# Four transposed quarters and sums behind them, in place of seven transposed operands

## The chip, the cores and the metric

One Trainium2 chip, one of its cores. The metric is the device time of one execution in microseconds; lower is better. A core has a matrix engine (TensorE, PE in the profile; its weight loads are PEld), VectorE (DVE), ScalarE (ACT) and GpSimd (POOL) for elementwise work, and SyncE (SP), whose queue issues most DMAs here.

## The reference

Two sequences, a prompt of 512 rows and a sample of 1024 rows, both 1024 wide, go through one encoder layer with the same weights. The part that matters here is the feed-forward half:

```python
h = _rmsnorm(x, norm_ffn_g[l])
u = _dwconv(h @ w_up[l], ffn_dw_w[l], ffn_dw_b[l])        # 1024 -> 2 x 2816
x = x + (jax.nn.silu(u[..., :D_FF]) * u[..., D_FF:]) @ w_down[l]
```

Everything is float32 in and out.

## The kernel before, in words

Every float32 product is made of three matmuls: each operand is split into a high part (rounded to fp32r, a cast on ACT) and a low part (what is left, one subtraction), and high x high, high x low and low x high are added up in PSUM.

For the sample, the product of the normed rows with `w_up` is made by a scheme of seven block products in place of eight. The rows are cut into four quarters: `rows[t, b]` holds row block `b` (128 rows) of half `t` (0 or 1) of the sequence, and `L` and `R` are its left and right 512 columns. With a11 = (t 0, L), a12 = (t 0, R), a21 = (t 1, L), a22 = (t 1, R), the seven left operands are

| operand | 1 | 2 | 3 | 4 | 5 | 6 | 7 |
|---|---|---|---|---|---|---|---|
| is | a11 | a12 | a12 - s2 | a22 | s1 = a21 + a22 | s2 = s1 - a11 | a11 - a21 |

For the matmuls each is needed transposed, as four chunks `c` of 128 columns by 512 rows, and split: `A[i, c] = (hi, lo)`.

In the kernel before, `scaled(i)` (L1091) forms the scaled row block and, for half 1, three of the four sums on DVE in row layout; `last_sum` forms the fourth, for two of the four row blocks at once and for the others later. `turned(i, get)` (L1121) then turns operand `i`: for each chunk, four PE transposes (one per row block) into one PSUM bank, the cast on ACT and the low part on DVE, both reading the bank (L1127 and, through the helper `sub`, L1074). Operands 1 and 2 are turned while the output projection of the layer's first half is still running (banks `u`); operands 4, 6, 7, 5 and 3 are turned between the first products of `w_up` (banks `t`, four of them).

`prod(out, j, i, ...)` (L1188) is the product of operand `i` with its partner of weight column `j`: four chunks of three matmuls, 12 in all, accumulating in a PSUM half. After each chunk it calls `next(between)`, through which the transposes come in between. `first` to `seventh` are these products with what goes on around them: for instance `sixth(j)` ends with an ACT copy of its result (`u2`), and `seventh(j)` goes on in the same bank. Before `sixth`, a matmul that writes a value to be overwritten (`armed`, L1257) and an ACT copy (L1394) put the result of product 1 into that bank; `arm()` does so for columns 0 and 1 in the course of `fourth(1)`. The banks they write take the place of the four turning banks, which must have been read by then.

The weight operands are made by `sums_up(j)` (sums on DVE) and `split_up(j, ...)` (L1165: a cast on ACT, the low part on POOL). All SBUF tiles come from a list of slots in fixed sizes (`Slots`; kinds q with 4 KB, c, h with 2 KB, d), handed out in the order in which they became free; a new tile waits for the last reader of the one that was in its slot.

The order of instructions on an engine is the compiler's scheduler's, by a model of time, apart from regions that say otherwise:

```python
by_hand = tc.manual_schedule(engines={mybir.EngineType.PE})
```

From L1352 to the end PE runs in the order in which the code emits, the other engines don't. The emitted order of the stage is: first(0), first(1), then second(0), fourth(0), second(1) with the 20 groups of four transposes in between, fourth(1) with the two armings, sixth(0), sixth(1), seventh(0), seventh(1), fifth(0), fifth(1), third(0), first(2), third(1) and so on; from column 2 on a loop over the 22 columns follows, then the down-projection.

Of the kernel before, what the change touches and what calls it, by code (L numbers as in the profile page):

```python
# [108 lines left out]
def tile_hybrid_encoder(ctx: ExitStack, tc: tile.TileContext, xs, rel_bias, norm_attn_g, w_in,  # L109
# [960 lines left out]
    def add(out, a, b, eng=None):  # L1070
        (eng or nc.vector).tensor_tensor(out, a, b, op=ALU.add)

    def sub(out, a, b, eng=None):
        (eng or nc.vector).tensor_tensor(out, a, b, op=ALU.subtract)  # L1074
# [16 lines left out]
    def scaled(i):  # L1091

        t, b = divmod(i - 4, 4)
        x = rows[t, b] = sb.tile([D])
        if t == 0:
            nc.vector.scalar_tensor_tensor(x[:], x1[i][:], rs2[:, i:i + 1], gFb[:], op0=ALU.mult, op1=ALU.mult)
            x1.pop(i)
            return
        for s in (R, L):
            nc.vector.scalar_tensor_tensor(x[:, s], x1[i][:, s], rs2[:, i:i + 1], gFb[:, s], op0=ALU.mult, op1=ALU.mult)  # L1100
        x1.pop(i)
        e = rows[0, b]
        s1 = rows["s1", b] = sb.tile([NT])
        s2 = rows["s2", b] = sb.tile([NT])
        add(s1[:], x[:, L], x[:, R])
        sub(s2[:], s1[:], e[:, L])
        sub(x[:, L], e[:, L], x[:, L])
        if i >= NB - 2:
            last_sum(b)

    def last_sum(b):
        sub(rows[0, b][:, L], rows[0, b][:, R], rows["s2", b][:])

    def block_rows(i, b):
        if i in (1, 2, 3):
            return rows[0, b][:, R if i == 2 else L]
        if i in (4, 7):
            return rows[1, b][:, R if i == 4 else L]
        return rows["s1" if i == 5 else "s2", b][:]

    def turned(i, get):  # L1121
        for c in range(4):
            held, ap = get()
            for b in range(4):
                nc.tensor.transpose(ap[:, b * P:(b + 1) * P], block_rows(i, b)[:, c * P:(c + 1) * P], ident[:])
            hi, lo = A[i, c] = (sb.tile([NT], F32R), sb.tile([NT], F32R))
            nc.scalar.copy(hi[:], ap)  # L1127
            sub(lo[:], ap, hi[:].bitcast(F32))
            held = None
            yield 0.0  # L1130
        key = {6: "s2", 5: "s1", 7: 1, 3: 0}.get(i)
        for b in range(4):
            rows.pop((key, b), None)

    def old_bank():
        b = bank("turn")
# [82 lines left out]
        for half in range(2):  # L1219
            load_up(j, half)  # L1220
    drain(side)
    for b in range(2):
        last_sum(b)
    split_up(0, 1, 2)
    out_blocks(NB - 2, 0)
    split_up(1, 1, 2)
# [42 lines left out]
    def second(j, between=None):  # L1269
        prod(st[j]["x"][:, L], j, 2, False, True, between)  # L1270
# [88 lines left out]
    def chain(*gens):  # L1359
        for g in gens:  # L1360
            yield from g

    def every(n, gen):

        for c in range(4):
            for _ in range((n * (c + 1)) // 4 - (n * c) // 4):
                next(gen, None)
            yield

    turns = chain(*(turned(i, turn_bank) for i in (4, 6, 7, 5, 3)))  # L1370
    firsts = []
    for j in range(2):
        st[j] = dict(x=wide())
# [16 lines left out]
    def arm():  # L1390
        for j in range(2):
# [438 lines left out]
```

## Time and profile before

| | |
|---|---|
| time, median of 3 runs | 1485.7 us (1485.24 to 1486.14) |
| the profiled execution's own time | 1484.85 us |
| its span (first to last instruction) | 1483.1 us |
| PE busy | 1468.5 us, 99% |
| DVE busy | 1118.2 us, 75% |
| ACT busy | 805.5 us, 54% |
| POOL busy | 770.7 us, 52% |

Times inside the execution count from the span's start. A row of the timeline gives the start, the duration, the engine, the line, the operation, what it writes and reads (slot kinds or tensors), and in brackets the idle time before it with what ended it. Matmuls overlap: the distance between two starts is what one costs, not its duration. A row of stretches gives, for each engine, its busy time and number of instructions, then the granted clock of PE, the DMA share and GB/s. The stage of the change lies at about 690 to 780 us.

### The profile page before, as it was taken

Reading aid. Unit: us, or ns where it says so; the run is one execution under the profiler, and the core shown is the slowest. Engines: PE = TensorE matmul, PEld = TensorE weight load, DVE = VectorE, ACT = ScalarE, POOL = GpSimd, SP = SyncE. Lnnn points to the kernel's source line nnn. Section 1 sums busy time; section 2 is a strip of 40 time slices with the busy share of each in tenths; the row PEclk is TensorE's granted clock in tenths of the full one; section 3 lists DMA queues with packets and bytes.
Section 4 is the critical chain, followed back from the end, with each engine's and each line's share of the span. In section 5 each row is a group of like instructions: output and inputs, shape, how many; then the busy total and the mean of one; then the engine's idle time right before and its main releaser. Section 6 shows DMA issues by size and latency. Waiting matters only on the chain.

```text
span 1483.1 us, 19870 instructions
## 1 busy us (share of the span) xinstructions
PE 1468.5 (99%) x6736; PEld 1212.0 (82%) x6736; DVE 1118.2 (75%) x1510; ACT 805.5 (54%) x1424; POOL 770.7 (52%) x689
## 2 busy tenths in 40 slices
PE   9999999999999999999999999999999999999998
PEld 7788887878888888788888888888888888888886
DVE  6877945648988888676868888888886856578774
ACT  7524555567778776653465545445544553433355
POOL 3564453338779766322336666666654251135546
PEclk9999999999999999999999999999999999999999
DMA  9554331844444454663214443333332494356644
GB/s 367 200 151 146 102 107 29 263 142 142 127 137 136 134 178 142 201 225 108 71 58 142 135 135 128 127 130 128 123 126 87 152 326 167 124 188 220 224 163 163
DMA packets 124626, 228.19 MB, mean 154 GB/s; under 512 B 20420, under 2 KB 45764, under 8 KB 124397
## 3 DMA queue, kind: packets, MB, share of 16 engines
q1 hardware_dynamic: 124092, 226.37, 46.6%
q8 instruction: 53, 0.87, 0.2%
q10 hardware_dynamic: 432, 0.56, 0.1%
q14 instruction: 49, 0.39, 0.1%
HBM read 166.83 MB, written 61.10 MB: 154 GB/s over the span
## 4 chain that ended last, share of the span: by engine, by line
PE 89%; DVE 3%; DMA 3%; ACT 2%; POOL 2%; issue 1%; SPq 0%; POOLq 0%; DVEq 0%; ACTq 0%
PE w L1194 8%; PE w L1196 8%; PE w L1195 8%; PE w L1528 7%; PE w L1527 7%; PE w L1526 7%; PE b L315 4%; PE b L317 4%; PE b L316 4%; PE u L315 4%; PE u L317 4%; PE u L316 4%; PE a L692 1%; PE a L650 1%; PE u L796 1%; PE u L798 1%
## 5 line engine op out<-in xcount | busy, mean ns | idle before, releaser
L163 POOL TENSOR_TENSOR q<-q,q 128x1024 fp32r<-128x1024 f32 x66 | 159.2, 2412 | 66.9 <-ACT q L162 42.8
L1074 POOL TENSOR_TENSOR q<-q,q 128x512 fp32r<-128x512 f32 x81 | 116.5, 1445 | 119.4 <-ACT q L1180 117.1
L1074 DVE TENSOR_TENSOR h<-h,h 128x512 fp32r<-128x512 f32 (+1 forms) x152 | 131.9, 897 | 57.6 <-ACT h L1082 23.4
L1526 PE MATMUL w<-h,h 128*128 128x512 f32 x432 | 168.0, 389 | 0.0
L1528 PE MATMUL w<-h,h 128*128 128x512 f32 x432 | 168.0, 389 | 0.0
L1527 PE MATMUL w<-h,h 128*128 128x512 f32 x412 | 160.3, 389 | 0.0
L1194 PE MATMUL w<-h,q 128*128 128x512 f32 x368 | 144.3, 392 | 0.7 <-ACT w L1267 0.4
L1196 PE MATMUL w<-h,q 128*128 128x512 f32 x368 | 143.2, 389 | 0.0
L1195 PE MATMUL w<-h,q 128*128 128x512 f32 x347 | 135.0, 389 | 0.0
L1074 POOL TENSOR_TENSOR h<-h,h 128x512 fp32r<-128x512 f32 (+1 forms) x38 | 53.5, 1411 | 142.4 <-ACT h L1509 117.5
L1082 ACT CAST h<-h 128x512 fp32r<-128x512 f32 x116 | 69.3, 620 | 104.4 <-DVE h L1074 25.8
L315 PE MATMUL b<-h,q 128*128 128x512 f32 x312 | 123.0, 395 | 1.4 <-ACT h L461 0.8
L317 PE MATMUL b<-h,q 128*128 128x512 f32 x312 | 122.5, 393 | 0.0
L316 PE MATMUL b<-h,q 128*128 128x512 f32 x312 | 122.3, 392 | 0.0
L315 PE MATMUL u<-h,q 128*128 128x512 f32 x272 | 106.8, 393 | 0.0
L316 PE MATMUL u<-h,q 128*128 128x512 f32 x272 | 106.8, 393 | 0.0
L317 PE MATMUL u<-h,q 128*128 128x512 f32 x272 | 106.7, 392 | 0.0
L162 ACT CAST q<-q 128x1024 fp32r<-128x1024 f32 x66 | 69.1, 1048 | 52.1 <-PE u L316 16.8
L352 DVE SCALAR_TENSOR_TENSOR c<-d,cvw,c 128x512 f32<-128x512 f32 x128 | 96.0, 750 | 1.6
L344 POOL TENSOR_TENSOR h<-h,h 128x512 f32<-128x512 f32 x62 | 81.6, 1318 | 27.5 <-ACT h L343 23.0
L1526 PEld LDWEIGHTS w<-h,h 128*128 128x128 f32 x432 | 81.1, 188 | 16.8
L1528 PEld LDWEIGHTS w<-h,h 128*128 128x128 f32 x432 | 81.1, 188 | 16.7
(474 smaller groups left out, 3990.3 us busy)
## 6 DMA issues: line engine op xcount, KB each, us to landing
q<-in_laid_w_up SPq DMA_DIRECT2D x88, 512.0 KB, 3.7
ga<-q SPq DMA_DIRECT2D x65, 256.0 KB, 2.2
h<-gap SPq DMA_DIRECT2D x57, 256.0 KB, 3.5
h<-ga SPq DMA_DIRECT2D x57, 256.0 KB, 3.5
h<-in_w_down SPq DMA_DIRECT2D x52, 256.0 KB, 3.4
q<-in_laid_w_in SPq DMA_DIRECT2D x22, 512.0 KB, 3.9
gap<-h SPq DMA_DIRECT2D x44, 256.0 KB, 3.2
q<-in_x_sample SPq DMA_DIRECT2D x15, 512.0 KB, 7.5
```

The costliest lines, as they stand in the source:

```text
L163: (nc.vector if dve else nc.gpsimd).tensor_tensor(lo[:], raw[:], hi[:].bitcast(F32), op=ALU.subtract)
L315: nc.tensor.matmul(out, whi[:, kc, :], hi[:], start=(kc == 0), stop=False)
L316: nc.tensor.matmul(out, whi[:, kc, :], lo[:], start=False, stop=False)
L317: nc.tensor.matmul(out, wlo[:, kc, :], hi[:], start=False, stop=(kc == KC - 1))
L352: nc.vector.scalar_tensor_tensor(acc[:], src(t), w(t), acc[:], op0=ALU.mult, op1=ALU.add)
L1074: (eng or nc.vector).tensor_tensor(out, a, b, op=ALU.subtract)
L1194: nc.tensor.matmul(out, whi[:, s], hi[:], start=(start and c == 0), stop=False, **go)
L1195: nc.tensor.matmul(out, whi[:, s], lo[:], start=False, stop=False, **go)
L1196: nc.tensor.matmul(out, wlo[:, s], hi[:], start=False, stop=(stop and c == 3), **go)
L1526: nc.tensor.matmul(out, sh[:, c], th[:], start=(p == 0 and not seeded), stop=False, **go)
L1527: nc.tensor.matmul(out, sh[:, c], tl[:], start=False, stop=False, **go)
L1528: nc.tensor.matmul(out, sl[:, c], th[:], start=False, stop=(p == NPAIR - 1), **go)
```

## The change

The rows are only scaled, no sums are formed in row layout. The four quarters are turned as they are (operands 1, 2, 4 and a21: 16 groups of four transposes instead of 28), and the three sums and the third operand's are formed afterwards on the turned chunks:

- Operands 1 and 2: the turned chunk is copied to SBUF by ACT and kept (`turn_raw`), ACT casts the copy, POOL makes the low part.
- `turned_second`: for each chunk, the right quarter is turned (operand 4: cast on ACT, low part on DVE from PSUM), then the left quarter; DVE forms s3 = a11 - a21 (operand 7) and s2 = a22 - s3 (operand 6) from PSUM; ACT casts s2, POOL makes its low part. The s2 of two chunks share a 4 KB slot.
- `last_sums`, in three parts: operand 7 split (ACT, DVE); operand 5 = s2 + a11 (DVE, in place) and split (ACT, POOL); operand 3 = a12 - s2 (DVE, in place) and split (ACT, POOL), for c > 0 with both parts in one 4 KB slot.

The groups of transposes come one after each chunk of second(0) and second(1). fourth(0) follows behind them. The first part of `last_sums` is emitted before fourth(0), the second after fourth(1), ahead of the splits of the weight operands 7 and 5, the third after sixth(1). From second(0) to the third part a region holds PE, DVE, POOL and ACT to the emitted order.

```diff
-        if t == 0:
-            nc.vector.scalar_tensor_tensor(x[:], x1[i][:], rs2[:, i:i + 1], gFb[:], op0=ALU.mult, op1=ALU.mult)
-            x1.pop(i)
-            return
-        for s in (R, L):
+        for s in (R, L) if i >= NB - 2 else (slice(0, D),):
             nc.vector.scalar_tensor_tensor(x[:, s], x1[i][:, s], rs2[:, i:i + 1], gFb[:, s], op0=ALU.mult, op1=ALU.mult)
         x1.pop(i)
-        e = rows[0, b]
-        s1 = rows["s1", b] = sb.tile([NT])
-        s2 = rows["s2", b] = sb.tile([NT])
-        add(s1[:], x[:, L], x[:, R])
-        sub(s2[:], s1[:], e[:, L])
-        sub(x[:, L], e[:, L], x[:, L])
-        if i >= NB - 2:
-            last_sum(b)
...
+    def turn_block(t, c, ap):
+        n, c = divmod(c, 4)
+        for b in range(4):
+            nc.tensor.transpose(ap[:, b * P:(b + 1) * P], rows[t, b][:, n * NT + c * P:n * NT + (c + 1) * P], ident[:])
+
+    def parts_of(i, c, src, eng, joint=False):
+        both = sb.tile([2, NT], F32R, among="q") if joint else None
+        hi, lo = A[i, c] = (Part(both, 0), Part(both, 1)) if joint else (sb.tile([NT], F32R), sb.tile([NT], F32R))
+        nc.scalar.copy(hi[:], src)
+        sub(lo[:], src, hi[:].bitcast(F32), eng)
 
     def turned(i, get):
         for c in range(4):
             held, ap = get()
+            turn_block(0, 4 * (i - 1) + c, ap)
+            raw = turn_raw[i, c] = sb.tile([NT])
+            nc.scalar.copy(raw[:], ap)
+            held = None
+            parts_of(i, c, raw[:], nc.gpsimd)
+            yield 0.0
...
+    def turned_second(get):
+        for c in range(4):
+            held, right = get()
+            turn_block(1, 4 + c, right)
+            parts_of(4, c, right, None)
+            yield
+            other, left = get()
+            turn_block(1, c, left)
+            if c % 2 == 0:
+                both = sb.tile([2, NT], among="q")
+            s3, s2 = sums[c] = sb.tile([NT]), Part(both, c % 2)
+            sub(s3[:], turn_raw[1, c][:], left)
+            sub(s2[:], right, s3[:])
+            held = other = None
+            parts_of(6, c, s2[:], nc.gpsimd)
+            yield
...
+    def last_sums():
+        for c in range(4):
+            s3, s2 = sums[c]
+            sums[c] = s2
+            parts_of(7, c, s3[:], None)
+            s3 = s2 = None
+        yield
+        for c in range(4):
+            raw = turn_raw.pop((1, c))
+            add(raw[:], sums[c][:], raw[:])
+            parts_of(5, c, raw[:], nc.gpsimd)
+            raw = None
+        yield
+        for c in range(4):
+            raw = turn_raw.pop((2, c))
+            sub(raw[:], raw[:], sums.pop(c)[:])
+            parts_of(3, c, raw[:], nc.gpsimd, c > 0)
+            raw = None
...
-    turns = chain(*(turned(i, turn_bank) for i in (4, 6, 7, 5, 3)))
+    turns = turned_second(turn_bank)
...
-    second(0, every(7, turns))
-    fourth(0, every(7, turns), True)
-    second(1, chain(every(8, turns)))
+    by_hand.__exit__(None, None, None)
+    by_hand = tc.manual_schedule(engines={mybir.EngineType.PE, mybir.EngineType.DVE, mybir.EngineType.Pool, mybir.EngineType.Activation})
+    by_hand.__enter__()
+    second(0, every(4, turns))
+    second(1, every(4, turns))
...
+    later = last_sums()
+    next(later)
...
+    fourth(0, None, True)
     fourth(1, chain(iter((None, None)), arm()), True)
     firsts.clear()
+    next(later)
     split_up(0, 7)
     split_up(1, 7)
     reserve(2)
...
     sixth(1)
+    next(later, None)
+    by_hand.__exit__(None, None, None)
+    by_hand = tc.manual_schedule(engines={mybir.EngineType.PE})
+    by_hand.__enter__()
```

More of the change, by code (lines that the diff above doesn't have):

```diff
@@ L1094, in scaled @@
         x = rows[t, b] = sb.tile([D])
-        if t == 0:
-            nc.vector.scalar_tensor_tensor(x[:], x1[i][:], rs2[:, i:i + 1], gFb[:], op0=ALU.mult, op1=ALU.mult)
-            x1.pop(i)
-            return
-        for s in (R, L):
+        for s in (R, L) if i >= NB - 2 else (slice(0, D),):
             nc.vector.scalar_tensor_tensor(x[:, s], x1[i][:, s], rs2[:, i:i + 1], gFb[:, s], op0=ALU.mult, op1=ALU.mult)
         x1.pop(i)
-        e = rows[0, b]
-        s1 = rows["s1", b] = sb.tile([NT])
-        s2 = rows["s2", b] = sb.tile([NT])
-        add(s1[:], x[:, L], x[:, R])
-        sub(s2[:], s1[:], e[:, L])
-        sub(x[:, L], e[:, L], x[:, L])
-        if i >= NB - 2:
-            last_sum(b)
[L1111 to L1119, printed above, removed]
+    turn_raw, sums = {}, {}
+    def turn_block(t, c, ap):
[7 more added lines that the diff above has]
+        sub(lo[:], src, hi[:].bitcast(F32), eng)
     def turned(i, get):
@@ L1123, in turned @@
             held, ap = get()
-            for b in range(4):
[L1125 to L1131, printed above, removed]
-        for b in range(4):
-            rows.pop((key, b), None)
+            turn_block(0, 4 * (i - 1) + c, ap)
[4 more added lines that the diff above has]
+            yield 0.0
+        if i == 2:
+            for b in range(4):
+                rows.pop((0, b))
+    def turned_second(get):
[14 more added lines that the diff above has]
+            yield
+        for b in range(4):
+            rows.pop((1, b))
+    def last_sums():
[16 more added lines that the diff above has]
+            raw = None
     def old_bank():
@@ L1221, in tile_hybrid_encoder @@
     drain(side)
-    for b in range(2):
-        last_sum(b)
     split_up(0, 1, 2)
```

## The prediction

> **What bounds the kernel now.** I read the page first: busy shares, then the chain that ended last.
>
> ```profile
> span 1483.1 us, 19870 instructions
> PE 1468.5 (99%) x6736; PEld 1212.0 (82%) x6736; DVE 1118.2 (75%) x1510; ACT 805.5 (54%) x1424; POOL 770.7 (52%) x689
> PE 89%; DVE 3%; DMA 3%; ACT 2%; POOL 2%; issue 1%; SPq 0%; POOLq 0%; DVEq 0%; ACTq 0%
> ```
>
> TensorE is the bound, so work taken off it is a gain unless it waits instead. The busy time by stretches around the edited stage (us; PE, PEld, DVE, ACT, POOL; clock; DMA):
>
> ```profile
> 700.00:720.00 20.00, 20.00 (x100) 16.59 (x98) 18.12 (x26) 7.79 (x16) 6.41 (x7) 1.00 0.16 52
> 720.00:740.00 20.00, 20.00 (x101) 16.62 (x100) 15.31 (x23) 8.83 (x16) 7.10 (x8) 1.00 0.31 104
> 740.00:760.00 20.00, 19.74 (x122) 16.67 (x121) 13.18 (x21) 14.61 (x28) 8.19 (x7) 1.00 0.19 61
> ```
>
> PE waits 0.26 us in these 60. Next, every transpose on the line that turns the sample's rows, and the PE timeline at the stage's corners:
>
> ```profile
> L1125 PE MATMUL t<-ident,q x40: 270/272/273, 737.8 to 753.3; 128*128 128x128 f32 x40
> L1125 PE MATMUL u<-ident,q x32: 270/272/275, 693.8 to 727.7; 128*128 128x128 f32 x32
> L1125 PE MATMUL t<-ident,h x32: 271/272/273, 740.9 to 750.2; 128*128 128x128 f32 x32
> L1125 PE MATMUL t<-ident,c x8: 272/273/273, 738.0 to 747.0; 128*128 128x128 f32 x8
> ```
> ```profile
> 731.66 0.39 PE L1194 MATMUL w<-h,q 128*128 128x512 f32 x1
> ...
> 737.56 0.39 PE L1196 MATMUL w<-h,q 128*128 128x512 f32 x1
> 737.79 0.38 PE L1125 MATMUL t<-ident,q 128*128 128x128 f32 x2
> ...
> 754.14 0.39 PE L1194 MATMUL w<-h,h 128*128 128x512 f32 x1
> ...
> 756.61 0.50 PE L1260 MATMUL w<-h 128*128 128x512 f32 x1 [0.26 <-DVE q L1074]
> ...
> 757.88 0.41 PE L1194 MATMUL w<-h,h 128*128 128x512 f32 x1
> ```
>
> The 32 in u are operands 1 and 2, the 80 in t (40+32+8) are operands 4, 6, 7, 5, 3. From 731.66 to 737.56 are 26 matmuls: 0.227 us each, so a product (12) costs 2.72. From 737.79 to 754.14 lie 80 transposes and 33 matmuls: (16.35 - 33 x 0.227) / 80 = 0.111 us each, 0.44 for a group of four.
>
> **The change part by part.**
>
> *Transposes.* Operands 4 and 7's source alone are turned, 32 instead of 80: 48 x 0.111 = 5.3 us off the bound engine. The 0.26 wait, for the last subtraction of the turns, goes too, because two products now lie between the turns and that spot. Together -5.6.
>
> *The row stage before 737.* Off DVE go 16 operations (four sums for each of four row blocks); eight low-part subtractions of operands 1 and 2 go to POOL, and ACT gets eight more casts. All of it lies beside a PE that is 20.00 of 20.00 busy, so I take 0. If that cover went, what is late is the last low part of operand 2: last transposes about 727.9, two ACT copies and one POOL subtraction more, about 730.7, wanted at 737.1. Six us of room; both ends of this cost are therefore 0. The 4 KB slots (the pairs of operand 3) change an address only: 0. SP issues the same DMAs; the one that waits in this stage is the load of the third weight column, for a slot whose last reader is a transpose:
>
> ```profile
> SPq L1151 <- PE t L1125: 13.8, 1, 13.8
> ```
>
> Fewer and earlier transposes can only bring that forward, and PE does not wait for it in any row above: 0.
>
> *The written order.* This is what can cost. Rates of the three engines, from their timelines in the same stage (a count xN runs back to back):
>
> ```profile
> 741.12 1.07 ACT L1127 CAST h<-t 128x512 fp32r<-128x512 f32 x2 [0.49 <-PE t L1125]
> 742.30 0.62 ACT L1180 CAST q<-h 128x512 fp32r<-128x512 f32 x1
> ...
> 747.42 0.63 ACT L1180 CAST q<-h 128x512 fp32r<-128x512 f32 x1
> ...
> 753.68 1.66 ACT L1180 CAST q<-q 128x512 fp32r<-128x512 f32 x3
> ```
> ```profile
> 712.33 1.78 DVE L1071 TENSOR_TENSOR h<-q 128x512 f32<-128x512 f32 x1
> ...
> 715.84 1.77 DVE L1074 TENSOR_TENSOR q<-q,q 128x512 f32<-128x512 f32 x1
> 717.53 1.77 DVE L778 SCALAR_TENSOR_TENSOR h<-h,h 128x512 f32<-128x512 f32 x1
> ...
> 748.56 1.89 DVE L1074 TENSOR_TENSOR h<-t,h 128x512 fp32r<-128x512 f32 x3 [0.32 <-ACT h L1127]
> ```
> ```profile
> 712.28 1.28 POOL L1074 TENSOR_TENSOR q<-q,q 128x512 fp32r<-128x512 f32 x1 [2.52 <-ACT q L1180]
> 715.45 3.30 POOL L1074 TENSOR_TENSOR h<-q,h 128x512 fp32r<-128x512 f32 x2 [1.89 <-PE c L797]
> ...
> 743.00 1.29 POOL L1074 TENSOR_TENSOR q<-h,q 128x512 fp32r<-128x512 f32 x1 [3.77 <-ACT q L1180]
> 748.12 1.28 POOL L1074 TENSOR_TENSOR q<-h,q 128x512 fp32r<-128x512 f32 x1 [3.83 <-ACT q L1180]
> 754.38 5.04 POOL L1074 TENSOR_TENSOR q<-q,q 128x512 fp32r<-128x512 f32 x4 [4.98 <-ACT q L1180]
> ```
>
> ACT: 0.48 us from one PSUM copy to the next (landing after 0.59), 0.52 from SBUF (0.62). DVE: (1.89 - 0.69) / 2 = 0.60 (0.69). POOL: (5.04 - 1.29) / 3 = 1.25 (1.29). From 0.03 to 0.08 at a hand-over; I use 0.04. A DVE operation with two SBUF inputs that meets POOL's subtraction takes 1.77 and POOL's two take 3.30 instead of 2.54: they take turns, about 1.85 a pair. The three DVE subtractions from PSUM at 748.56 run in 1.89 although POOL works from 748.12, so those do not collide.
>
> With these I walk the four lists in the order that the code writes. *First wait.* For each block c ACT must cast the right quarter, DVE make its low part, the third and the second sum, ACT cast that sum, and only then comes ACT's next block: 0.59 + 0.60 + 0.60 + 0.69 + 0.52 + four hand-overs = 3.2 us, where PE gives a block every 2 x (0.44 + 0.68) = 2.2. PE's turns end at 746.1, but the low part of operand 4's last block lands at 749.0, and fourth(0) wants it at 748.3: 0.7 us. *Second.* The second sum of the last block lands at 750.2, ACT's cast of it at 750.9, then four casts of operand 7. By my count of 2 KB slots five are free there, so the fourth cast takes the slot of a third sum that DVE has still to read (753.5). Only behind it stand the two copies that arm the accumulators; the first lands at 754.6 and sixth(0) was due at 752.7: 2.0. *Third.* DVE ends operand 7's low parts at 754.9, adds, ACT casts, POOL starts operand 5's first low part at 756.6. POOL's list has four of these ahead of the low part of weight operand 7, which today is made long before, at 743.00 and 748.12. DVE meanwhile has three adds and four subtractions with two SBUF inputs, so five pairs of about 1.85 follow: 765.3. sixth(0) and sixth(1) end at 760.1; seventh(0) first waits for ACT's copy of the sixth product (behind four casts of operand 5 and four of weights), 1.7, then two matmuls later for POOL, 3.1. After that POOL makes a weight part in 1.25 to 1.85 where PE needs 2.72 for a product, and fifth and third find theirs. What waits behind PE at seventh(0) is the rest of the loop.
>
> Sum: -5.6 + 0.7 + 2.0 + 1.7 + 3.1 = +1.9 us. If POOL and DVE never met, the same walk gives 0.7 + 1.25 + 0.45 + 1.5 = 3.9 of waits and -1.7: the lower bound of a binding order. The upper one adds the wait of first(2), behind four low parts of operand 3 on POOL, at most one pair, 0.9: +2.8. I take the collision, since it has rows in the same kind of operation, and 0 for first(2).
>
> The profiled execution took 1484.85, 0.85 below the median; differences go onto the median, 1485.7 + 1.9 = 1487.6. A measurement of this kernel tells about 0.2% (3.0 us) from no change, so the forecast is "no change".
>
> **The clock.** A stop of PE seldom comes alone in this trace. The stop at 626 and the granted clock of the stretches behind it:
>
> ```profile
> 625.59 0.48 PE L650 MATMUL a<-q,h 128*128 128x256 f32 x2
> 627.56 0.49 PE L706 MATMUL a<-h,h 128*128 128x512 f32 x1 [1.49 <-ACT h L694]
> ```
> ```profile
> 628.00:632.00 4.00, 3.97 (x14) 2.30 (x14) 4.00 (x9) 3.54 (x8) 1.29 (x2) 0.70 0.96 329
> 632.00:636.00 4.00, 4.00 (x20) 3.39 (x20) 3.10 (x5) 3.48 (x7) 1.67 (x1) 0.87 1.02 390
> ```
>
> It cost 4 x 0.30 + 4 x 0.13 = 1.7 us beyond the stop. The Trainium skill, "TensorE: Matmul & The Clock Gate" (Part 1, the HAM clock gate), has PE fall to half clock after an idle window of about 3.4 us and speaks against this change, whose two stops at seventh(0) make 4.8 almost together. By that rule the sum would be +3.6; with a window longer than my stops it stays +1.9. This trace has a drop after only 1.49 of full stop, so the measurement is the stricter of the two.
>
> **The rivals.**
> 1. *The clock drops at seventh(0)* (slower). Place: 760 to 765; price 1.7; it decides once the stops there pass about 1.5 us close together. For it: the rows at 626. Against: a single occurrence, with sparse work around it. 1485.7 + 1.9 + 1.7 = 1489.3.
> 2. *POOL and DVE do not collide there* (or the lists interlock better): -1.7, 1484.0. For: operations from PSUM pass POOL freely. Against: the adds and the last subtractions read SBUF twice.
> 3. *The weight parts do not queue behind the sums* (faster), and nothing collides: seventh(0) finds all ready, 0.7 + 1.25 of waits are left: -3.6, 1482.1; with no wait at all 1480.1. For: today they are made at 743.00 and 748.12. Against: the region orders POOL as written, and there they come after operand 5.
>
> **How the numbers follow.** Forecast 0.38, rival 1 0.25, rival 2 0.17, rival 3 0.20. Faster by over 0.2%: rival 3 and a little of 2, 0.23. Slower: rival 1 and the forecast's upper end (first(2) waits, a stop more), 0.31. Between: 0.46. The range 1481.5 to 1490.5 holds the forecast, rivals 1 and 2 and most of rival 3, and leaves out 1480.1 and a drop of the clock with further waits; the forecast's own range is 1484.0 to 1488.5.
>
> **What would show it.** Right: 64 transposes on the turning lines instead of 112; PE waits at fourth(0), sixth(0), seventh(0) of about 0.7, 2.0 and 4.8, the last named to POOL's subtraction; DVE's adds stretched to about 1.8. Rival 1: clock under 1.00 near 765. Rival 2: adds at 0.7. Rival 3: POOL makes weight operand 7 before operand 5. Wrong altogether: a wait of PE before 737 or a new one in the loop from 780 on.

## The result: 8.8 us slower, and the profile after

The changed kernel takes 1494.6 us (median of 6 runs, 1493.8 to 1496.9) against 1485.8 for the kernel before on the same chip: a ratio of 1.006, 95% interval [1.0047, 1.0073]. The forecast was 1487.6. The profiled execution took 1493.76.

The page of the kernel after, span and busy shares, and the first three lines of the table of what PE waited for (us in total, times, longest):

```profile
span 1491.9 us, 19791 instructions
PE 1466.7 (98%) x6688; PEld 1207.0 (81%) x6688; DVE 1114.5 (75%) x1488; ACT 808.4 (54%) x1432; POOL 810.5 (54%) x709
```
```profile
PE w L1222 <- ACT h L1302: 6.5, 2, 5.9
PE w L1222 <- ACT w L1424: 1.7, 1, 1.7
PE w L1222 <- ACT w L1293: 1.6, 4, 0.5
```

PE has 48 matmuls fewer (6688 for 6736), as the diff says, and the span is 8.8 us longer. PE's own rows show where (the bracket is the idle time before the row and what ended it):

```profile
749.00 0.49 PE L1222 MATMUL w<-h,h 128*128 128x512 f32 x1 [0.25 <-ACT h L1109]
749.73 0.50 PE L1223 MATMUL w<-h,h 128*128 128x512 f32 x1 [0.23 <-DVE h L1074]
...
755.37 0.50 PE L1222 MATMUL w<-h,h 128*128 128x512 f32 x1 [1.68 <-ACT w L1424]
...
767.00 0.79 PE L1222 MATMUL w<-h,q 128*128 128x512 f32 x1 [5.87 <-ACT h L1302]
...
768.44 0.63 PE L1222 MATMUL w<-h,q 128*128 128x512 f32 x1
768.87 0.63 PE L1223 MATMUL w<-h,q 128*128 128x512 f32 x1
```

These are fourth(0), sixth(0) and seventh(0). After the last one matmuls are 0.43 us apart, not 0.227: the clock has dropped. The stretches there (PE, PEld, DVE, ACT, POOL, clock, DMA):

```profile
760.00:764.00 4.00, 1.12 (x5) 0.58 (x4) 4.00 (x3) 1.87 (x4) 4.00 (x4) 0.91 0.00 0
764.00:768.00 4.00, 1.00 (x2) 0.83 (x3) 1.80 (x2) 2.16 (x5) 4.00 (x3) 0.50 0.00 0
768.00:772.00 4.00, 4.00 (x15) 3.19 (x14) 0.00 (x0) 2.54 (x5) 4.00 (x5) 0.73 0.15 18
```

The reading that serves for all kernels below is the *offset*: the start of a product's first matmul, this kernel's profiled execution minus that of the kernel before, in us.

| offset at | first(0) | sixth(0) | seventh(0) | seventh(1) | third(0) | first(2) | 785 us of before | end of the products |
|---|---|---|---|---|---|---|---|---|
| after | +0.40 | -2.51 | +3.64 | +5.20 | +5.41 | +5.54 | +5.54 | +8.87 |

So: 0.4 lost ahead of first(0), 2.9 gained from there to sixth(0), 6.15 lost up to seventh(0), 1.6 more in the slow clock behind it, 0.3 to first(2), and 3.3 in the loop. What PE waits for at seventh(0) is ACT's copy of the sixth product (L1302), at 766.36. The rows of ACT, DVE and POOL ahead of it:

```profile
760.74 1.13 ACT L1208 CAST q<-q 128x512 fp32r<-128x512 f32 x2
765.84 0.62 ACT L1208 CAST q<-q 128x512 fp32r<-128x512 f32 x1 [3.96 <-DVE h L1074]
766.36 0.58 ACT L1302 COPY h<-w 128x512 f32<-128x512 f32 x1
```
```profile
755.49 3.59 DVE L1071 TENSOR_TENSOR h<-q,h 128x512 f32<-128x512 f32 x4
759.00 6.80 DVE L1074 TENSOR_TENSOR h<-h,q 128x512 f32<-128x512 f32 x4
```
```profile
756.96 6.63 POOL L1074 TENSOR_TENSOR h<-h,h 128x512 fp32r<-128x512 f32 x4 [3.94 <-ACT h L1109]
763.55 3.38 POOL L1074 TENSOR_TENSOR q<-h,q 128x512 fp32r<-128x512 f32 x2
```

The copy stands behind a cast of a weight operand (the foreign cast, below) whose slot DVE's last subtraction still reads, and that subtraction ends at 765.80 because from 757.30 on DVE's and POOL's operations take turns at 1.7 us each. The row of the four adds (755.49) hides this: one by one, the first three start 0.60 us apart, and the fourth, beside POOL's first low part, takes 1.70. By the emitted order the cast is `split_up(1, 3)`, which the code emits behind the region; the scheduler put it inside. This is read from the order of ACT's list, and e2 tests it.

### The profile page after: what moved, and what is told of

It is laid out like the page before. It is cut to its first block, busy times and chain, and to the rows that moved or that the text cites. A ratio compares the mean times of both kernels' runs of the same rounds, so it can differ in the third digit from the quotient of the medians.

```text
span 1491.9 us, 19791 instructions
## 1 busy us (share of the span) xinstructions
PE 1466.7 (98%) x6688; PEld 1207.0 (81%) x6688; DVE 1114.5 (75%) x1488; ACT 808.4 (54%) x1432; POOL 810.5 (54%) x709
## 4 chain that ended last, share of the span: by engine, by line
PE 85%; DVE 7%; DMA 2%; issue 2%; ACT 2%; POOL 2%; SPq 0%; POOLq 0%; DVEq 0%; ACTq 0%
PE w L1222 7%; PE w L1224 7%; PE w L1223 7%; PE w L1562 7%; PE w L1564 7%; PE w L1563 7%; PE b L315 4%; PE b L317 4%; PE b L316 4%; PE u L315 4%; PE u L317 4%; PE u L316 4%; PE u L796 1%; PE u L797 1%; PE u L798 1%
## 5 line engine op out<-in xcount | busy, mean ns | idle before, releaser
L1074 POOL TENSOR_TENSOR q<-q,q 128x512 fp32r<-128x512 f32 x81 | 120.7, 1499 | 111.8 <-ACT q L1208 111.8
L1074 POOL TENSOR_TENSOR h<-h,h 128x512 fp32r<-128x512 f32 (+1 forms) x51 | 75.4, 1484 | 147.7 <-ACT h L1545 105.6
L1222 PE MATMUL w<-h,q 128*128 128x512 f32 x346 | 137.1, 396 | 7.8 <-ACT h L1302 6.5
L1223 PE MATMUL w<-h,q 128*128 128x512 f32 x346 | 135.3, 391 | 0.0
L1224 PE MATMUL w<-h,q 128*128 128x512 f32 x346 | 135.2, 391 | 0.0
```

Source lines behind the costliest of these rows:

```text
L1222: nc.tensor.matmul(out, whi[:, s], hi[:], start=(start and c == 0), stop=False, **go)
L1223: nc.tensor.matmul(out, whi[:, s], lo[:], start=False, stop=False, **go)
L1224: nc.tensor.matmul(out, wlo[:, s], hi[:], start=False, stop=(stop and c == 3), **go)
```

## The experiments

Offsets come from each run's one profile; they shift by what varies ahead of the stage (first(0) at +0.1 to +3.0), so differences within a row count.

| kernel | median us | ratio [95%] | first(0) | sixth(0) | seventh(0) | seventh(1) | third(0) | first(2) | 785 | end |
|---|---|---|---|---|---|---|---|---|---|---|
| e1 free order | 1495.0 | 1.0058 [1.0043, 1.0073] | +1.60 | +7.72 | +7.71 | +9.16 | +9.31 | +9.31 | +9.31 | +10.07 |
| e2 cast inside | 1493.1 | 1.0051 [1.0034, 1.0068] | +1.14 | -1.78 | -0.04 | +3.69 | +4.94 | +5.07 | +5.07 | +7.99 |
| e3 weights 7 early | 1489.6 | 1.0024 [1.0013, 1.0035] | +0.48 | -3.53 | -1.29 | +0.03 | +1.76 | +1.89 | +1.89 | +5.07 |
| e4 both | 1491.3 | 1.0034 [1.0023, 1.0045] | +0.46 | -3.55 | -1.30 | -1.17 | +2.26 | +3.99 | +4.01 | +5.98 |
| e5 dummies | 1496.8 | 1.0070 [1.0055, 1.0085] | +0.41 | -2.50 | +11.27 | +11.27 | +11.27 | +11.41 | +11.41 | +11.81 |
| e6 low parts 5 on DVE | 1499.1 | 1.0087 [1.0072, 1.0102] | +0.40 | -2.50 | +2.26 | +4.83 | +10.64 | +12.29 | +12.30 | +13.37 |
| e7 reordered | 1491.6 | 1.0037 [1.0022, 1.0051] | +2.96 | -1.83 | -1.74 | +1.87 | +6.88 | +7.04 | +7.04 | +9.05 |
| e8 pipelined | 1501.6 | 1.0104 [1.0089, 1.0119] | +0.09 | +3.07 | +6.57 | +8.31 | +8.34 | +8.34 | +9.78 | +17.86 |
| e9 no sums | 1507.9 | 1.0143 [1.0126, 1.0160] | +2.92 | -1.66 | -1.57 | -1.57 | -0.07 | +0.06 | +0.06 | +24.24 |
| e10 no adds | 1490.8 | 1.0032 [1.0021, 1.0043] | +0.75 | -2.16 | -1.06 | +0.34 | +2.43 | +2.56 | +2.56 | +5.67 |
| e11 full order | 1498.3 | 1.0074 [1.0055, 1.0093] | +0.91 | -1.23 | +0.34 | +3.11 | +4.84 | +4.84 | +12.03 | +13.46 |
| e12 early loads | 1512.8 | 1.0180 [1.0166, 1.0194] | +2.52 | -1.48 | -1.39 | +2.28 | +4.07 | +4.07 | +5.48 | +30.44 |
| e13 two sums | 1503.9 | 1.0127 [1.0112, 1.0143] | +0.47 | -0.82 | -0.77 | -0.77 | -0.08 | +0.05 | +0.05 | +17.95 |
| e14 fewer turns | 1485.9 | 1.0000 [0.9991, 1.0009] | +0.23 | -0.43 | +1.19 | +1.19 | +1.19 | +1.19 | +1.19 | +0.96 |
| e15 fewer parts | 1482.8 | 0.9981 [0.9971, 0.9990] | +0.70 | -2.32 | -2.33 | -2.33 | -2.33 | -2.33 | -2.33 | -2.29 |

### Is it the written order? (e1, e2, e3, e4, e7)

e1 gives three engines back to the scheduler:

```diff
-    by_hand = tc.manual_schedule(engines={mybir.EngineType.PE, mybir.EngineType.DVE, mybir.EngineType.Pool, mybir.EngineType.Activation})
+    by_hand = tc.manual_schedule(engines={mybir.EngineType.PE})
```

> The changed kernel with the region holding PE alone to the emitted order, so DVE, ACT and POOL are ordered by the scheduler as before; sums, transposes and slots as in the change. Theory A (the written order makes the stop at seventh(0)): the stop of 6.1 us goes or falls under 2, the clock stays at 1.00, and the time falls by 5 us or more, to 1484 to 1489. Rival B (the sums on the turned chunks are too much serial work for DVE, ACT and POOL in any order): the stop stays above 4 and the time within 2 us of 1494.6.

```profile
748.74 0.41 PE L1104 MATMUL t<-ident,q 128*128 128x128 f32 x2 [2.42 <-DVE q L1074]
759.14 0.79 PE L1223 MATMUL w<-h,h 128*128 128x512 f32 x1 [6.35 <-DVE h L1074]
```

The order is not the cause as such: freed, the kernel is as slow, and the stop stands at fourth(0), where DVE made sums and differences at 1.7 us each ahead of the low part that PE wanted.

e2 emits `split_up(1, 3)` at the end of the region instead of behind it; e3 emits `split_up(0, 7)` and `split_up(1, 7)` before second(0) instead of behind the sums; e4 does both.

> The changed kernel with split_up(1, 3) emitted inside the region, behind the third part of the sums. Its cast stood on ACT ahead of the copy of the sixth product and waited for a slot that DVE's last subtraction had to free. Theory A: the copy lands near 762 instead of 766.9, seventh(0) starts there and waits again, for POOL's low part of weight operand 7 at about 765.4; seventh(0) ends 1.3 us earlier, 2.5 if the clock holds: 1492 to 1493.5. Rival C (the cast was harmless, POOL alone sets the stop): 1494.6, within 0.5.

> The changed kernel with split_up(0, 7) and split_up(1, 7) emitted before second(0), the foreign cast left where it is. Theory A: POOL has the weight's low part long before, but PE still waits for the copy behind the cast, so the stop shrinks by 1 us at most: 1493.5 to 1494.6. Rival C (POOL's queue alone): the stop goes, 1488 or less.

> Both moves together. Theory A: nothing is left at seventh(0) but ACT's copy, 0.5 to 1 us after the sixth product; no drop of the clock; third(0) starts about 2 us earlier than in the kernel before instead of 5.4 later. If the 3.3 us lost later in the loop are a consequence of the stop, 1484 to 1485; if they come from the order that the scheduler makes there, 1487 to 1488. Rival B: a stop above 3 us stays and the time is above 1490.

PE's stops from seventh(0) on, of e2, e3 and e4 in turn:

```profile
763.32 0.50 PE L1222 MATMUL w<-h,q 128*128 128x512 f32 x1 [1.48 <-ACT h L1302]
766.05 0.80 PE L1224 MATMUL w<-h,q 128*128 128x512 f32 x1 [2.00 <-POOL q L1074]
779.18 0.50 PE L1222 MATMUL w<-h,q 128*128 128x512 f32 x1 [1.06 <-DVE w L1071]
```
```profile
762.07 0.50 PE L1222 MATMUL w<-h,q 128*128 128x512 f32 x1 [1.99 <-ACT h L1302]
776.00 0.50 PE L1222 MATMUL w<-h,q 128*128 128x512 f32 x1 [1.09 <-DVE w L1071]
```
```profile
762.06 0.50 PE L1222 MATMUL w<-h,q 128*128 128x512 f32 x1 [1.95 <-ACT h L1302]
776.50 0.50 PE L1222 MATMUL w<-h,q 128*128 128x512 f32 x1 [3.27 <-DVE w L1071]
```

e2 shows the forecast's own pair (1.7 for the copy, 3.1 for POOL) at 1.48 and 2.00: the foreign cast had hidden POOL's wait behind ACT's and lengthened it. e3, with POOL's weight parts out of the way, is the best order found; it is 3.2 us slower than before all the same, and came between its two expected cases. In it DVE and POOL did not take turns. DVE, POOL and ACT of e3:

```profile
755.38 2.49 DVE L1071 TENSOR_TENSOR h<-q,h 128x512 f32<-128x512 f32 x4
757.79 2.48 DVE L1074 TENSOR_TENSOR h<-h,q 128x512 f32<-128x512 f32 x4
```
```profile
756.84 4.56 POOL L1074 TENSOR_TENSOR h<-h,h 128x512 fp32r<-128x512 f32 x1 [3.73 <-ACT h L1109]
```
```profile
761.43 0.59 ACT L1302 COPY h<-w 128x512 f32<-128x512 f32 x1 [1.86 <-POOL h L1074]
```

DVE's four adds and four subtractions ran back to back at 0.61 us each, all with two SBUF inputs. POOL's first low part, begun among them, took 4.56 us and ended 1.1 us behind the last of them; its next ones took about 1.3. The copy that seventh(0) needs waited 1.86 us for this low part. e4 shows the same, with 4.57. So here the collision cost POOL and not DVE; why DVE gave way in the changed kernel and not in these two is not shown.

In e4 DVE was free earlier and the scheduler used that for the sums of column 2, ahead of the sum that third(0) waits for: 3.27.

e7 goes further: weight operands 7 and 5 split in the gaps of the turns, the arms' copies ahead of operand 7's casts, the sums' second part behind sixth(0), the third behind sixth(1).

> The same transposes, sums and products as the change in another written order: the splits of the weight operands 7 and 5 in the gaps of the turns, the arming copies ahead of operand 7's casts, the splits of operand 3's weights before the sums' second part, that part behind sixth(0) and the third behind sixth(1). Theory A (the saving of 5.6 us is there, and order alone took it): no stop above 1 us before third(0), which starts 3 to 5 us earlier than in the kernel before; time 1481 to 1486. Rival B (the sums are too much serial work near here in any order): the stops move on to fifth(0) or third(0) and add up to more than 5 us; 1488 or more.

```profile
767.95 0.80 PE L1226 MATMUL w<-h,q 128*128 128x512 f32 x1 [3.45 <-ACT h L1306]
```

No stop above 0.25 us is left up to seventh(0), whose offset is 4.7 below first(0)'s; then the sums, moved back, stop the next product for 3.45, and fifth(0) and third(0) for 1.20 and 0.74.

### The clock and the division of work (e5, e6)

e5 puts 24 dummy matmuls ahead of seventh(0) to keep the clock up; e6 moves operand 5's low parts from POOL to DVE.

```diff
+    for _ in range(24):
+        armed(st[0]["wy"][:, L])
     seventh(0, None, False)
```

> The changed kernel with 24 more matmuls of 0.227 us between sixth(1) and seventh(0), into a half bank that nothing uses yet (product 5 starts it afresh later). They fill 5.4 us of the stop of 6.1 and put nothing off. Theory A (the granted clock falls because PE stands still, and costs 1.5 us): the clock stays at 1.00 between 760 and 772, seventh(0) starts at 767 as before and runs at 0.227 a matmul, the time falls by 1.5 to 1493.1 (0.6 either way). Rival (the slow matmuls after the stop come from their operands, not from the clock): no change, 1494.6.

> The changed kernel with the low parts of operand 5 made by DVE instead of POOL. Theory A (DVE's adds and subtractions and POOL's low parts block each other): the adds and last subtractions take 0.7 each instead of 0.9 to 1.7, DVE is done with the last subtraction near 763 instead of 765.8, POOL has the weight parts of operand 7 by 758, the stop at seventh(0) falls to about 3: 1490 to 1492. Rival (no collision; four more DVE operations in front of the last subtraction): the stop stays, 1494.6 or above.

```profile
767.00 7.79 PE L1286 MATMUL w<-h 128*128 128x512 f32 x24 [5.88 <-ACT h L1302]
```

e5 did not do what it was made for: the dummies wrote the other half of the same bank pair and waited for the same copy, so they came behind the stop and cost 7.8 us. It says nothing on what the clock costs. e6 makes it worse by 4.5 at the end: its stop at seventh(0) is 4.51, at third(0) 5.53 for DVE. The adds took 0.69 as expected, but DVE stood 0.74 us for ACT's cast ahead of each of the four low parts, so that its subtractions began at 763.65 instead of 759.00. The chain through ACT got longer; that DVE has less room than POOL is not shown.

### What the sums cost (e9, e10)

```diff
# e9: nothing of last_sums is computed
+            A[7, c] = A[6, c]
...
+            A[5, c] = A[6, c]
...
+            A[3, c] = A[4, c]
# e10: only the eight two-operand sums are left out
-            add(raw[:], sums[c][:], raw[:])
...
-            sub(raw[:], raw[:], sums.pop(c)[:])
+            sums.pop(c)
```

> The changed kernel without its last part: s1, the third operand's difference and the splits of operands 7, 5 and 3 are left out, and the products 7, 5 and 3 read the parts of operands 6 and 4 instead. The transposes saved stay saved. Theory A (the loss comes from this work behind the last transposes): no stop above 0.7 us from seventh(0) to first(2), the arm's 1.7 us at sixth(0) goes too, first(2) starts 3.5 to 5 us earlier than before, end 1480 to 1484. Rival B (the loss comes from the weight operands' parts and from the order around them): a stop of 2 us or more stays at seventh(0) or third(0), end 1488 or more.

> The changed kernel with only the eight two-operand sums of the second and third part left out (DVE's 3.6 and 6.8 us behind the turns); the casts and low parts of operands 7, 5 and 3 are made all the same, from the unsummed chunks. Theory A1 (DVE's sums and their collision with POOL's low parts set the stop at seventh(0)): POOL's four low parts of operand 5 take 1.3 us each instead of 1.66, start some 2 us earlier, and the cast that u2 stood behind is free by 761; stop at seventh(0) under 1.5 us, end 1486 to 1489. Rival C (POOL's queue of low parts alone sets it: four of operand 5 ahead of two of the weights): the stop stays at 3 us or more, end 1491 or more.

From first(0) to fifth(1) (at seventh(1)'s offset in all three) e9 gains 4.5, e10 0.4, and the changed kernel loses 4.8. So the work behind the turns costs 9.3 us there: 5.2 for the eight sums (with the 1.56 of the slow clock, which e10 does not have), 4.1 for the casts and low parts of operands 7, 5 and 3 with the slots that they wait for. In e10 seventh(0) waits 0.80 and 1.01 instead of 5.87, in e9 not at all. Theory A holds for seventh(0) to fifth(1). Past that it does not: third(0) still waits for DVE, 1.34 in e9 and 1.93 in e10; first(2) of e9 comes 2.9 us earlier against first(0), not 3.5 to 5; and neither end came as expected, 1490.8 for e10 and 1507.9 for e9. What e9 loses at the end lies in the loop, in code that was not edited: other slots are free there, and PE waits in almost every column, above all for ACT's copy of the first product:

```profile
PE w L1216 <- ACT w L1287: 12.6, 16, 1.8
```

### Can an order hide them? (e8, e11, e12)

All three pipeline the turns (ACT's cast of s2 behind the next block's first cast), form s1 on DVE inside the turns and give operand 3's low parts to DVE. e11 writes the order of all engines on to first(2); e12 gives operand 5's pairs the 4.3 KB slots and issues the loads of columns 2 and 3 before the turns.

> Same operations as the changed kernel, another order. In the turns the cast and low part of s2 of a chunk are emitted behind the next chunk's cast, so that ACT's cast of operand 4 no longer stands behind them; s1 = s2 + a11 is formed on DVE inside the turns; POOL makes operand 5's low parts from there on, DVE operand 3's; the weight parts of operand 7 are split before the turns, those of 5 and 3 behind; DVE keeps the emitted order through first(2), so that the sums of column 2 come behind the y sums. Theory A (the loss is the sums' serial chain on DVE and POOL behind the last transposes, and what stands in it): the chain is about 8 us shorter after the turns, so the stops at sixth, seventh and third shrink to under 2 us together; third(0) starts 1 to 4 us earlier than in the kernel before and the end comes at 1483 to 1487. Rival B (DVE, ACT and POOL lack capacity in this stage, whatever the order): the stop comes back at another product with 3 us or more, and the time is 1489 to 1493, as in the orders tried so far.

> The order of e8 without what stopped it there: the arms' copies stand ahead of the last casts of operand 5, three of the four pairs of operand 5 lie in 4 KB slots that are free from the start of the turns (operand 3's pairs in 2 KB slots instead), and the written order of all engines goes on to first(2), so that no cast of column 2 can be put among the casts of the turns; p5, the y sums and the sums of column 2 in the order in which PE needs them. Theory A (the loss is the serial chain of sums behind the turns and waits for slots in it, not too little capacity): stops at sixth, seventh and third together under 3 us, third(0) starts 1 to 4 us before the kernel before, end 1483 to 1487. Rival B (DVE, ACT and POOL lack capacity in this stage, in any order): stops of 5 us or more together again, end 1489 or later.

> e11 with the foreign casts kept out: in e8 and e11 two casts of column 3's weights, emitted in the loop, were put among the casts of the turns by the scheduler (into 4.3 KB slots that the row blocks free), and one of them held ACT 2.7 us for its DMA. Here operand 5's pairs take those slots, so these casts come behind the region, and the loads of columns 2 and 3 are issued before the turns; the four differences of operand 3 are formed one ahead of their casts on DVE; the depthwise steps of columns 0 and 1 stand where their banks are complete. Theory A (serial chain with foreign waits in it, not capacity): the stop at sixth(0), 3.5 us in e11, is under 0.7 us, seventh and third stop under 2 us together, first(2) starts no later than in the kernel before (offset -3 to +1), end 1483 to 1488. Rival B (capacity): stops of 4 us or more together stay, end 1490 or later.

The turns did get shorter, but each kernel stopped elsewhere: e8 8.66 us at sixth(0), e11 3.54 there, 2.62 at seventh(1) and 4.46 at fifth(2), e12 1.68 at sixth(0) and 3.50 at seventh(1). In e8 and e11 a cast stood in the turns that the region does not contain; by the listing of ACT's instructions it is one of column 3, for whose load ACT waited (ACT of e8):

```profile
749.84 0.62 ACT L1212 CAST c<-q 128x512 fp32r<-128x512 f32 x1 [2.75 <-DMA q<-in_laid_w_up]
```

In e12 these casts are gone, and the collision is still there. DVE, then POOL:

```profile
759.21 1.78 DVE L1074 TENSOR_TENSOR h<-h,h 128x512 fp32r<-128x512 f32 x1
760.92 1.78 DVE L1074 TENSOR_TENSOR h<-h,q 128x512 f32<-128x512 f32 x1
762.62 1.78 DVE L1074 TENSOR_TENSOR h<-h,h 128x512 fp32r<-128x512 f32 x1
...
766.89 0.69 DVE L1074 TENSOR_TENSOR h<-h,h 128x512 fp32r<-128x512 f32 x1 [0.21 <-ACT h L1109]
```
```profile
756.99 5.15 POOL L1074 TENSOR_TENSOR c<-h,c 128x512 fp32r<-128x512 f32 x3
762.10 3.43 POOL L1074 TENSOR_TENSOR q<-q,q 128x512 fp32r<-128x512 f32 x2
```

The same subtraction takes 0.69 with POOL idle (766.89) and 1.78 beside it (759.21). No order tried came under 3.2 us slower; that none exists is not shown. e12's and e8's further loss lies in the loop, as in e9.

### What are fewer transposes worth at all? (e13, e14, e15)

All three start from the kernel before. e13 turns operands 1, 2, 4, 6, 7 and forms 5 and 3 by one DVE instruction each while the turned s2 lies in PSUM. e14 only leaves out 32 transposes: operands 5 and 3 take casts and low parts from the banks of 6 and 7, all else is made as before. e15 leaves out those casts and low parts too.

```diff
# e13, in turned()
+            if i == 6:
...
+                add(one[:], ap, one[:])
+                sub(two[:], two[:], ap)
# e14, in turned()
+            if i in (6, 7):
+                hi, lo = A[{6: 5, 7: 3}[i], c] = (sb.tile([NT], F32R), sb.tile([NT], F32R))
+                nc.scalar.copy(hi[:], ap)
+                sub(lo[:], ap, hi[:].bitcast(F32))
# e15: the last two lines left out again; the products 5 and 3 read the parts of 6 and 7
```

> The kernel before, with operands 1, 2, 4, 6 and 7 turned (20 groups of four, 32 transposes fewer: 3.55 us at 0.111) and operands 5 = s2 + a11 and 3 = a12 - s2 formed on DVE while the turned s2 lies in PSUM, one instruction of 0.7 us each beside the turns; ACT keeps copies of the turned operands 1 and 2 and casts them; POOL makes the low parts of 5 and 3 behind the turns; the scheduler's order, only PE by hand. Theory A (the loss of the change is the two-step chain from SBUF behind the turns): no stop above 0.7 us from fourth(1) to third(0), first(2) starts 2.5 to 3.5 us earlier than in the kernel before, end 1482 to 1484.5. Rival B (any sum on turned chunks loads DVE and POOL too much here): stops of 3 us or more together, end 1486 or later.

> The kernel before with 32 transposes left out and nothing put in their place: operands 5 and 3 take their casts and low parts from the banks in which operands 6 and 7 were turned; row sums, casts and low parts are all made as before. It leaves out the turning of operands 5 and 3 alone. Theory A: 32 x 0.111 = 3.55 us less on PE, first(2) starts 3.2 to 3.8 us earlier and the end is 2 us or more earlier: 1481.5 to 1484. Rival B (what is saved in this stage is given back in the loop, whose first columns then wait for DVE and ACT): first(2) 3 us or more earlier, but the end within 1 us of the kernel before: 1485 to 1487.

> e14 without the casts and low parts of operands 5 and 3 as well: products 5 and 3 read the parts of operands 6 and 7, the slots stay taken. ACT has 8 casts and DVE 8 low parts of 0.6 to 0.7 us fewer in the turns, PE the same 32 transposes fewer as e14. Theory A (in the kernel before, the turns have two equal bounds, PE's transposes and DVE's and ACT's parts): the stop of 2.73 us at the arms falls under 0.5 us, no clock is lost, first(2) starts 3 to 3.8 us earlier than in the kernel before, and with little lost in the loop the end is 1481.5 to 1483.5. Rival B (the saving is lost elsewhere anyway): first(2) earlier by 3 us, the end within 1 us of the kernel before or later.

This is the result that matters most. e14, with 3.55 us less for PE and nothing added, is as fast as the kernel before. PE of e14 at the arms, and the stretches there:

```profile
756.21 0.47 PE L1264 MATMUL w<-h 128*128 128x512 f32 x1 [2.73 <-DVE q L1074]
```
```profile
752.00:756.00 4.00, 1.48 (x7) 0.87 (x5) 2.93 (x5) 3.23 (x7) 4.00 (x4) 1.00 0.15 18
756.00:760.00 4.00, 3.79 (x12) 2.97 (x13) 0.06 (x1) 1.18 (x2) 0.80 (x1) 0.72 0.75 244
```

The wait that the kernel before shows at this spot with 0.26 us, for the same last low part, is 2.73 here. DVE of e14 shows why:

```profile
744.40 8.61 DVE L1074 TENSOR_TENSOR h<-t,h 128x512 fp32r<-128x512 f32 x14 [0.31 <-ACT h L1127]
753.77 0.69 DVE L1074 TENSOR_TENSOR q<-t,d 128x512 fp32r<-128x512 f32 x1 [0.76 <-ACT d L1127]
754.77 0.69 DVE L1074 TENSOR_TENSOR d<-t,h 128x512 fp32r<-128x512 f32 x1 [0.31 <-ACT h L1131]
755.38 0.68 DVE L1074 TENSOR_TENSOR q<-t,q 128x512 fp32r<-128x512 f32 x1
```

Fourteen low parts back to back, 0.615 us each: DVE, with ACT's casts ahead of it, ends at 756.06, where the kernel before ended at 756.56 with 32 transposes more. So beside PE's transposes a second chain, ACT's casts and DVE's low parts, ends as late, and PE's 99% showed one of the two.

That this second chain is at its full rate is not shown. From 740.95 on DVE makes twenty low parts and one other subtraction; at 0.615 us each they would end at about 753.9, an estimate. It stood 1.95 us between them, each time for a cast of ACT. ACT's list has casts of weight operands among these, and one of them held it for 1.89 us. ACT of e14, then ACT and DVE of the kernel before:

```profile
742.26 0.62 ACT L1184 CAST q<-q 128x512 fp32r<-128x512 f32 x1 [1.89 <-DVE q L1074]
```
```profile
755.25 0.59 ACT L1127 CAST q<-t 128x512 fp32r<-128x512 f32 x1
```
```profile
755.87 0.69 DVE L1074 TENSOR_TENSOR q<-t,q 128x512 fp32r<-128x512 f32 x1 [1.35 <-ACT q L1127]
```

In the kernel before, too, the last low part waited for ACT, which made three casts of weight operands (753.68 to 755.25) ahead of that last cast. So the 0.26 us may come from the order of ACT's list as well as from too little room. Another place for those weight casts, or transposes emitted faster than one group after each chunk, was not tried.

What was left of the saving went into the clock behind the stop (0.72): 1.6 us between the offsets of sixth(0) and sixth(1). With the parts gone as well (e15) the stop is 0.57 (under 0.5 was expected), the clock stays, and 3.0 of the 3.55 us arrive at the end: 1482.8, ratio 0.9981. So it is this chain that took the saving; whether by its rate or by its order stays open. Rival B of e14 predicted the time, but not for its reason: nothing is given back in the loop, which takes 0.2 us off the offset in e14 and adds 0.04 in e15.

e13 shows the middle way: in the stage it keeps 1.2 us of the 3.55 (stops of 1.51 and 0.48 for DVE's low parts in the turns), and loses 18 in the loop, where PE waits for ACT's first copy fifteen times, 12.1 us in all, as in e9. Its end lies where rival B put it, but the stops in the stage come to less than the 3 us of that case; it decides nothing.

## Why the prediction was wrong

Three terms of the sum failed. The stop at seventh(0), put at 4.8, cost 6.15, because the walk took ACT's list as closed and a cast emitted behind the region held ACT for 3.96 us. The clock, put at 0, cost 1.56. The loop, put at 0 without a reason, cost 3.33. Point by point, by the steps of the prediction and the offsets of the changed kernel:

| step | predicted | measured |
|---|---|---|
| row stage, start of first(0) | 0 | +0.40 |
| first(0) to sixth(0): -5.6 +0.7 +2.0 | -2.9 | -2.91 |
| seventh(0), stop (with sixth(1)) | +4.8 | +6.15 |
| clock behind it | 0 | +1.56 |
| to 785 us of before | 0 | +0.34 |
| loop | 0 | +3.33 |
| sum | +1.9 | +8.87 |

- *Transposes and the two early waits* were right: 64 transposes are left, and the waits are 0.48 at fourth(0) and 1.68 at sixth(0) for 0.7 and 2.0 (from start to start, 0.90 and 1.84 more than matmuls 0.227 apart). The low part of operand 4's last block, the slot ahead of the arms and the queue of casts came as walked.
- *seventh(0)*: mis-sized by 1.35, and the wait that ended the stop was another one: it is named to ACT's copy, not to POOL. The collision itself came about as forecast: DVE's last subtractions took 1.70 each, as did the last add, though the three adds before it ran at 0.60. POOL's first weight part ended at about 765.3, as walked. What the walk did not have was the foreign cast ahead of the copy: I took the region's list as closed, and it holds only the order of what is in it. With that cast moved (e2), the two waits of the walk appear, 1.48 for the copy and 2.00 for POOL.
- *The clock*, rival 1, happened and was put at 1.7: 1.56. In the text of the forecast it was 0. The Trainium skill, "TensorE: Matmul & The Clock Gate" (Part 1), names an idle window of about 3.4 us. As a bound on a stop it does not hold here, and the measurement decides: the stop of 1.99 in e3 was followed by a drop, that of 1.95 in e4 was not (the stretch behind each, e3's first). Over the seventeen traces, from 100 us of the span on, a drop followed none of the 299 stops shorter than 1.48 us, 12 of the 31 from 1.48 to 2.56, and all 14 longer ones (stops are idle times of PE over 0.15 us that begin at full clock; a drop counts when it begins in the stop or within 3.5 us behind it). So the row at 626 was no exception, but its length alone did not decide: stops of 1.88 and 2.42 (e1) and of 2.56 (e8) passed without a drop. Of the two stops that the prediction put at seventh(0), 1.7 and 3.1, the second is longer than any that passed.

```profile
764.00:768.00 4.00, 4.00 (x13) 3.15 (x12) 0.95 (x2) 3.00 (x6) 4.00 (x4) 0.63 0.00 0
```
```profile
764.00:768.00 4.00, 4.00 (x19) 3.33 (x18) 0.78 (x2) 3.23 (x7) 4.00 (x4) 1.00 0.00 0
```

- *The loop*, taken as 0, is the largest miss. Most of its 3.3 us comes with four stops:

```profile
802.06 0.50 PE L1222 MATMUL w<-h,c 128*128 128x512 f32 x1 [0.36 <-ACT w L1293]
...
819.35 0.50 PE L1222 MATMUL w<-h,q 128*128 128x512 f32 x1 [0.65 <-ACT h L1302]
...
822.83 0.50 PE L1222 MATMUL w<-h,q 128*128 128x512 f32 x1 [0.47 <-ACT w L1293]
...
976.67 0.50 PE L1222 MATMUL w<-h,q 128*128 128x512 f32 x1 [0.44 <-ACT w L1293]
```

  The offset rises by 0.65, 0.93, 0.75 and 0.71 over them, the first two matmuls behind each included; 0.6 comes back at a stop that the kernel before has as well, the rest comes in steps of 0.1. At 818.19 ACT casts a weight that waits 0.97 us for DVE ahead of the copy that PE needs. The order is the scheduler's. Kernels with the layout of the kernel before (e14, e15) lose nothing there; those close to the changed kernel lose 0.4 to 3.3, e8 loses 8, and e9, e12 and e13 lose 18 to 25. What decides it was not settled. A new wait in the loop is what the prediction itself named as a sign of being wrong altogether.
- *The premise*, "TensorE is the bound, so work taken off it is a gain unless it waits instead", is what fell. I read the 0.26 us wait at the arms as something to be gained. e14 and e15 show that it was the mark of a second chain: with the casts and low parts as they are made there, 3.55 us less of PE gain nothing, and with sixteen of them fewer they gain 3.0. The change did take such work off the turns, which is why the gain showed at sixth(0), but it put it behind the turns, where six products of 2.72, 16 us up to fifth(0), must cover a chain of casts, sums and low parts that took longer in every order tried.
- Rivals 2 and 3: no collision (rival 2) was wrong for the subtractions and the last add. Weight parts out of POOL's queue (rival 3) did not happen; e3 made it happen and gave 1489.6, not 1482.1. DVE there ran as in rival 2, but POOL was held in its place, and the copy's wait of 1.99, the sum at third(0), the clock and the loop remained.

## What to carry to other kernels

Before taking work off an engine that is 99% busy, look at its shortest waits: one of 0.3 us in the stage named the chain that was next. How much that chain allows is found by leaving the work out with nothing put in its place (e14), and its own list shows whether it is busy throughout or held by an order; both before anything is built. Work that moves from before a stage to behind it must be costed against the cover there, and with the collision of DVE and POOL on both sides: here a DVE operation with two SBUF inputs took 1.7 us instead of 0.6 beside POOL, or POOL's took 4.56 instead of 1.3 (e3). The order written by hand for a region bound only what was emitted in it; instructions from behind were put among them, with their waits (e8, and by e2 the changed kernel). And a change in one stage can cost in code that was not edited: 3.3 us in the loop here, 18 to 25 in e9, e12 and e13.

## What the runs showed of the hardware

- DVE subtractions of 128x512 from two SBUF tiles start 0.60 us apart, and one alone takes 0.69 with POOL idle (e12, 766.89). Beside POOL's subtractions they took 1.70 to 1.78 (e12, 759.21); in e3 and e4 eight such operations ran beside POOL's at 0.61 each, and POOL's took 4.56. Those that read PSUM ran at 0.60 to 0.62.
- The granted clock fell after each PE stop of 2.6 us or more (14 of 14), after 12 of the 31 between 1.48 and 2.56, and after none of 299 shorter ones. Apart from the end of the span, each slow stretch lasted 3.41 or 6.83 us, at 0.5. In e3, e14 and the changed kernel it cost 1.3 to 1.6 us beyond the stop.
- The stop near 628 us, ahead of the stage, is 1.49 in the kernel before and 1.03 (e3) to 2.56 (e8) in the others, though no edit touches it; offsets at first(0) of 0.1 to 3.0 come from ahead of the stage.
